# FFN-out in passes of 8, 8 and 6 units, and operands fetched by the places left for them

## The chip, the core and the metric

The kernel runs on one NeuronCore of a Trainium2 chip. The core has a matrix engine (TensorE, PE in the profile), a vector engine (VectorE, DVE), a scalar engine (ScalarE, ACT), a general engine (GpSimd, POOL) and a sequencer that issues most of the DMAs (SyncE, SP). Each works through its own queue in order, and semaphores tie the queues together. The metric is device time in microseconds (us) for one call. Working memory (SBUF) holds the operands, PSUM the sums of the matmuls.

## The reference

One decoder layer on 512 tokens, all in float32, with a residual stream x of width 2048:

```python
h = rmsnorm(x, attn_norm_g); proj = h @ w_in            # 2048 -> 9216
...                                                      # spatial gating, stick-breaking attention
x = x + merged @ w_o                                     # x1
h = rmsnorm(x, ffn_norm_g); hid = h @ w_ffn_in           # 2048 -> 2 * 5632
x = x + (jax.nn.silu(gate) * up) @ w_ffn_out             # 5632 -> 2048, x2
x = x + jax.nn.sigmoid(rmsnorm(x, ple_norm_g) @ w_ple_gate) * (p @ w_ple)
```

The change touches the last three of these products: FFN-in (`w_ffn_in`), FFN-out (`w_ffn_out`) and the gate (`w_ple_gate`).

## The kernel before

Activations lie transposed: features over the 128 partitions, tokens along the row. A *unit* is 256 features by 512 tokens, 1024 float32 in each partition. A product sums over units of its input and makes one *pair* (256 output features by 512 tokens) at a time; `j` counts the pairs of an output, eight of them for a width of 2048. FFN-in sums over 8 units and makes 44 pairs (`m`); FFN-out sums over 22 units of the hidden layer, and as the operands of 22 units don't fit in SBUF it does so in passes (`PASSES`, L33): 8, 7 and 7 units, each pass making all eight pairs, with the partial sums kept in DRAM (`spill["sum", j]`) between passes. The gate sums over 8 units again.

To get float32 accuracy from the faster float32r matmul, each operand is split into a high part (copied by ACT) and the rest (subtracted by DVE), and three matmuls make one product (`mm3`, L274; L280, L281 and L282 are its three matmuls): high by high, high by rest, rest by high. A unit's contribution to a pair is made in one of two forms:

- P, plain: four blocks of weights by two halves of the unit, 12 matmuls with 512 columns.
- S, after Strassen and Winograd: seven products of sums of quarters, 21 matmuls with 256 columns. FFN-in uses a variant of it for all its pairs but the first (L692, 14 matmuls, 7 of 512 and 7 of 256 columns).

The sums of weights that S needs are made on the fly: one by an accumulating DMA that POOL issues (L347), two by DVE (L359); ACT (L343) and DVE (L340) split the weights. Units go in doubles (`doubles`, L411) where two neighbours of one kind start at an even position; a unit left over goes singly, with weights of half the size. In FFN-out the second pass starts at unit 8 and the third at 15.

The operand of an S unit has seven quarters: the four plain ones and three sums. It takes one of eight *places* (3584 columns, high and rest) in an arena called `parts`; a P unit takes two blocks of 1024. Raw units, weights that land and whatever else is loaded live in a second arena, `wholes`, 13,312 columns. An S operand can be used as a plain one while its sums are not there yet: `PLAIN_UNTIL` (L34) says for each unit of a pass for how many pairs it is taken plain. In the kernel before, the first four units are taken plain for one pair and the others for two; in the gate and in FFN-in all units are taken plain for the first pair only.

A `Form` is such an operand in the making. `late_form` (L573) loads the unit, multiplies it by a gain where there is one (`gained`, L503, two ACT instructions at L504), and goes on with `plain_first` (L514): it splits the four plain quarters (L270 on ACT, L271 on DVE), gives the raw unit back, and later loads the same unit a *second* time, multiplies it by the gain again, makes the sums (`tt`, L509) and splits them. `all_first` (L551), which the first stage of the kernel uses, does all that from one load: the sums are made beside the plain quarters and split a little later.

What is fetched and built when is decided at every `tick` (L199), which comes twice in a double, and once in a single. A tick fetches one of the next three forms in `builds`, if there is room in `wholes`; it starts the next form if it has arrived and a place for it is left; and otherwise it fetches the second load of a form:

```python
        urgent = [f for f in seconds if f.used]
        for f in list(builds)[: 0 if urgent else AHEAD]:
            if not f.there and f.ready() and fits([(wholes, 1024, "old")]):
                f.fetch()
                break
        if builds and builds[0].ready() and builds[0].arrived() and fits(builds[0].sizes):
            builds.popleft().step()
        elif seconds and fits([(wholes, 5 * 256, "old")]):
            (urgent or seconds)[0].fetch_second()
```

The forms of the next pass enter `builds` ahead of the last pair of a pass, and those of the gate (`gs`) ahead of the last pair of the third pass. In that last pair each unit's place is given back when the unit has been used. The scheduler of the language then sets the order on every queue from dependences and estimated times; loads can be moved far ahead by it.

In the third pass a pair ends with its sum being added to the partial sum (L801), scaled (L1225), added to x1 (L1439) and written to DRAM as x2 (L1440); the third normalisation adds up its squares (L957, L961). The gate's operands are loaded from there (L500).

Of the kernel before, what the change touches and what calls it, by code (L numbers as in the profile page):

```python
# [19 lines left out]
P = 128  # L20
# [3 lines left out]
KU = D // (2 * P)  # L24
HID = 5632
KH = HID // P
# [3 lines left out]
EPS = 1e-6  # L30

OUT = "SSSSPPPP"
PASSES = 8, 7, 7  # L33
PLAIN_UNTIL = 1, 1, 1, 1, 2, 2, 2, 2  # L34
GATE = "SSSSSPPP"
PLACE = 7 * 256

AHEAD, WAIT = 3, 2
# [28 lines left out]
def hybrid_layer(  # L67
# [93 lines left out]
    def fits(sizes):  # L161

        before = parts.holes, wholes.holes
        parts.holes, wholes.holes = list(parts.holes), list(wholes.holes)
        try:
            for arena, n, how in sizes + [(wholes, 1024, "low")]:
                arena.take(n, how)
            return True
        except ValueError:
            return False  # L170
        finally:
            parts.holes, wholes.holes = before
# [26 lines left out]
    def tick():  # L199

        clock[0] += 1
        last, units = traced()[-1], dict(newest)
        urgent = [f for f in seconds if f.used]
        for f in list(builds)[: 0 if urgent else AHEAD]:
            if not f.there and f.ready() and fits([(wholes, 1024, "old")]):
                f.fetch()
                break
        if builds and builds[0].ready() and builds[0].arrived() and fits(builds[0].sizes):
# [3 lines that stand above are left out]
        while waiting and waiting[0][0] <= clock[0]:  # L212
            heapq.heappop(waiting)[2]()
        for i in reversed(traced()):
            if i is last:
                break
            if i.engine in units:
                tc.add_manual_dep(
                    i, units[i.engine],
                    mybir.DependencyInfo(mybir.DependencyClass.NoSync,  # L220
                                         mybir.DependencyReason.DATA),
                    reason="in its place among the units")
# [288 lines left out]
    def twice(x):  # L511
        return x.unsqueeze(1).to_broadcast([P, 2, 256])

    def plain_first(form, raw, gain=None):  # L514


        x = form.operand()
        split_into(x[:, 0:4, 0], x[:, 0:4, 1], cut(raw.f()))
        give(raw)
        form.at_plain = True  # L520
        seconds.append(form)
        yield
        while not form.second_arrived():
            yield
        w = form.second
        b = cut(w.f())
# [24 lines left out]
    def all_first(form, raw):  # L551


        b, s, v = cut(raw.f()), take(768, "old"), take(256, "old")
        t, x = cut(s.f()), form.operand()
        split_into(x[:, 0:4, 0], x[:, 0:4, 1], b)
        tt(t[:, 2], b[:, 3], b[:, 2])
        tt(v.f(), b[:, 3], b[:, 1])
        tt(t[:, 0], t[:, 2], b[:, 1])
        tt(t[:, 1], t[:, 0], b[:, 0], ALU.add)  # L560
        give(raw)
        form.at_plain = True
        yield
        yield
        split_into(x[:, 4:7, 0], x[:, 4:7, 1], t)
        give(s)
        yield
        while not form.used:
            yield
        split_into(x[:, 3, 0], x[:, 3, 1], v.f())  # L570
        give(v)

    def late_form(src, ready=always, gain=None, far=False):  # L573

        def steps(form):
            form.blocks = (parts.take(2 * PLACE, "place"),)
            w = form.raw()
            if gain:  # L580
                gained(w.f(), w.f(), *gain)
            yield
            yield from plain_first(form, w, gain)
            return form.operand()

        return Form("S", steps, [(parts, 2 * PLACE, "place")] + [(wholes, 1024, "low")], ready,
                    src, far)

    def strassen_form(src, ready=always, gain=None, raw=PLACE):

# [213 lines left out]
                    s = h[:, i * T : (i + 1) * T]  # L804
                    nc.vector.tensor_tensor(out=s, in0=s, in1=ps, op=ALU.add)

    def pair(forms, last=False, plain=None, parts_done=None, at=0, home=lambda: None,
             doubled=0):

        plain = plain or (0,) * len(forms)
        kinds = "".join("P" if n else f.kind for f, n in zip(forms, plain))
        p = Pair(kinds, home, doubled)
        for k, n in doubles(kinds, at):
            slot, ws = next_weights()
            fs = forms[k : k + n]
            p.add(kinds[k], ws, [f.plain() if plain[k] else f.get() for f in fs])
            for f, left in zip(fs, plain[k : k + n]):
                if left == 1:  # L820
                    f.use_plain()
                if last:
                    f.free()
            slots.append(slot)
            if parts_done and k + n == kinds.find("P"):
                last_parts(p, forms[k + n :], parts_done)
                break
        return p

    def plain_left(n, j, until=PLAIN_UNTIL):  # L830

        return tuple(max(0, u - j) for u in until[:n])

    def kinds_of(forms_kinds, j, until=PLAIN_UNTIL):
        return "".join("P" if left else k
                       for k, left in zip(forms_kinds, plain_left(len(forms_kinds), j, until)))

    def last_parts(p, forms, done):

# [435 lines left out]
    def plan_rest():  # L1275
        for j in range(KU):
            for b in "ba":
                plan((w_up_a if b == "a" else w_up_b)[j], "PPPP")
        for j in range(KU):
            plan(w_o[j], OUT)  # L1280
        for j in range(3, KU):
            planned.append((w_ple[j].rearrange("p (b c) -> p b c", b=4), 1, "P"))
        for m in range(KH):
            plan(w_ffn_in[m], ("S" if m else "P") * KU)
        at = 0
        for n in PASSES:
            for j in range(KU):
                plan(w_ffn_out[j], kinds_of("S" * n, j), at)
            at += n
        for j in range(KU):  # L1290
            plan(w_gate[j], GATE if j else "P" * KU)

    def y_form(c, i):
        return plain_form((lambda: y_a[i]) if c == "a" else lambda: load(y_spill[i]),
# [68 lines left out]
             for j in range(KU)}  # L1363
    there = set()

    def spilled_form(kind, n, j, gain=None):
        return (late_form if kind == "S" else plain_form)(
            lambda size=1024: load(spill[n, j], size), lambda: (n, j) in there, gain, far=True)

    fs = [spilled_form("S", "x1", j, (g_ffn, j)) for j in range(KU)]  # L1370
    raw = deque([load(xT[0])])
    for j in range(KU):
        if j < KU - 1:
# [14 lines left out]
    for j in range(5, 8):  # L1388
# [4 lines left out]

    spill.update({("hid", u): tc.dram_tile([P, 1024], F32, name=nm("hid"))
                  for u in range(KH // 2)})
    hs = [spilled_form("S", "hid", u) for u in range(KH // 2)]
    def hidden(m, o):
        g = o[:, :T]
        nc.vector.tensor_tensor(out=g, in0=g, in1=row2, op=ALU.mult)  # L1399
# [6 lines left out]

    for m in range(KH):
        if m == KH - 1:
            builds.extend(hs[: PASSES[0]])
        o = pair(fs, last=m == KH - 1, plain=(0 if m else 1,) * KU, doubled=7).out()  # L1410
        if m == 0:
            row2 = norm2.row()
        st = Staged(hidden(m, o))
        st.step()
        if m == KH - 1:
            st.get()
# [1 line left out]
    gs = [spilled_form(k, "x2", j, (g_ple, j)) for j, k in enumerate(GATE)]  # L1418
    norm3 = Norm()
    at = 0  # L1420
    for c, n in enumerate(PASSES):
        units, first = hs[at : at + n], at
        at += n
        for j in range(KU):
            if j == KU - 1:
                builds.extend(hs[at : at + PASSES[c + 1]] if c + 1 < len(PASSES) else gs)
            before = load(spill["sum", j]) if c else None
            x1 = load(spill["x1", j]) if c == len(PASSES) - 1 else None
            pr = pair(units, last=j == KU - 1, plain=plain_left(n, j), at=first)
            if before is None:  # L1430
                nc.sync.dma_start(out=spill["sum", j], in_=pr.out())
                continue
# [14 lines left out]
    for j in range(KU):  # L1447
# [18 lines left out]
            nc.sync.dma_start(out=outT[j][:, a:b], in_=s)  # L1466

        if j == KU - 1:
            pair(gs, parts_done=finish)
        else:  # L1470
            o = pair(gs, plain=(0 if j else 1,) * KU).out()
            row3 = norm3.row()
            finish(o, 0, 2 * T)
            give(e, x2)
# [87 lines left out]
```

## Time and profile before

| what | us |
|---|---|
| median of 3 runs | 2722.21 (2721.26 to 2723.8) |
| profiled execution, its own time | 2724.13 |
| its span, first to last instruction | 2722.2 |
| PE busy | 2668.2 (98%) |
| DVE busy | 2204.5 (81%) |
| ACT busy | 1405.6 (52%) |
| POOL busy | 477.3 (18%) |

Busy time is the time in which at least one instruction of the engine was running; matmuls overlap, so that their durations add up to more. The rows of a group give the engine, the line, the tiles written and read with their shape, how many there were, then their busy time in us and the mean duration of one in ns, then the idle time of the engine ahead of them and who ended it. "A <- B" in the waits means that engine and line A waited for B. A row of the chain of work gives start, duration and what ran. Along the time axis FFN-in runs from about 1190 to 2055 us, the passes of FFN-out from 2055, 2222 and 2364, and the gate from about 2525 to the end.

### The profile page before, as it was taken

What the parts mean: (1) busy time and instruction counts of PE and PEld (TensorE: products, weight loads), DVE (VectorE), ACT (ScalarE), POOL (GpSimd) and SP (SyncE); (2) the same over time, 40 slices, a digit from 0 to 9 for tenths busy, and PEclk for the clock granted to TensorE, in tenths of its full rate; (3) what the DMA queues carried; (4) which work ended last, traced back from release to release, by engine and by line L of the source; (5) the groups of instructions that cost most, each with busy time, mean ns of one, the idle gap of its engine ahead of it and who ended that gap; (6) DMA issues with size and microseconds to landing.
All of it is one profiled execution on the core that took longest, in us unless ns stands there. A gap on an engine that the chain in (4) does not pass through costs nothing.

```text
span 2722.2 us, 44416 instructions
## 1 busy us (share of the span) xinstructions
PE 2668.2 (98%) x16334; PEld 2374.5 (87%) x16334; DVE 2204.5 (81%) x3685; ACT 1405.6 (52%) x2174; POOL 477.3 (18%) x566
## 2 busy tenths in 40 slices
PE   8999999999999999999999999999999999989899
PEld 7888888888998889978888888888888999989698
DVE  8687878788887566679989898989889778789776
ACT  7656565655554343385444444444445444444643
POOL 0232323232210000011111111111111102111110
PEclk9999999999999999999999999999999999999899
DMA  7676777777775466688888888787878879889884
GB/s 227 155 189 167 189 167 190 167 200 180 178 189 193 131 181 200 172 268 209 205 229 201 207 195 215 195 209 195 206 193 263 245 223 283 252 238 277 253 234 124
DMA packets 305883, 557.74 MB, mean 205 GB/s; under 512 B 26752, under 2 KB 155648, under 8 KB 305664
## 3 DMA queue, kind: packets, MB, share of 16 engines
q1 hardware_dynamic: 242496, 447.52, 51.1%
q0 software_dynamic: 63168, 107.37, 24.7%
q8 instruction: 128, 2.10, 0.3%
q14 instruction: 91, 0.75, 0.1%
HBM read 507.61 MB, written 47.19 MB: 204 GB/s over the span
## 4 chain that ended last, share of the span: by engine, by line
PE 86%; DVE 6%; DMA 3%; ACT 2%; issue 2%; POOL 1%; SPq 0%; DVEq 0%; ACTq 0%; POOLq 0%
PE ps L692 40%; PE ps L281 13%; PE ps L282 13%; PE ps L280 13%; PE small L692 4%; DVE wlo L340 2%; DVE parts L271 1%; DVE out L751 1%; DMA wholes<-hid 1%; DMA wholes<-x 1%; PE small L1158 1%; ACT whi L343 1%; PE small L1033 1%; DVE wholes L509 1%; PE small L1108 1%
## 5 line engine op out<-in xcount | busy, mean ns | idle before, releaser
L343 ACT ACTIVATE whi<-wholes 128x1280 fp32r<-128x1280 f32 (+3 forms) x960 | 876.1, 927 | 805.6 <-DVE wholes L359 273.7
L692 PE MATMUL ps<-parts,whi 128*128 128x512 f32 x3384 | 1135.5, 398 | 3.3 <-ACT out L789 2.6
L340 DVE TENSOR_TENSOR wlo<-wholes,whi 128x1280 fp32r<-128x1280 f32 (+3 forms) x960 | 984.3, 1059 | 86.5 <-ACT whi L343 86.0
L281 PE MATMUL ps<-parts,whi 128*128 128x256 f32 (+1 forms) x2799 | 881.2, 315 | 11.1 <-DVE parts L271 10.8
L280 PE MATMUL ps<-parts,whi 128*128 128x256 f32 (+1 forms) x2782 | 869.5, 315 | 21.3 <-ACT parts L270 15.7
L282 PE MATMUL ps<-parts,wlo 128*128 128x256 f32 (+1 forms) x2799 | 878.6, 315 | 0.6 <-DVE wlo L340 0.6
L692 PEld LDWEIGHTS ps<-parts,wlo 128*128 128x128 f32 x3384 | 635.8, 188 | 142.0 <-issue 1.0
L692 PE MATMUL ps<-parts,wlo 128*128 128x256 f32 x3384 | 671.2, 279 | 0.0
L281 PEld LDWEIGHTS ps<-parts,whi 128*128 128x128 f32 x2799 | 536.5, 192 | 51.7 <-DVE parts L271 15.1
L280 PEld LDWEIGHTS ps<-parts,whi 128*128 128x128 f32 x2782 | 531.3, 192 | 57.2 <-ACT parts L270 18.5
L282 PEld LDWEIGHTS ps<-parts,wlo 128*128 128x128 f32 x2799 | 535.6, 192 | 33.1 <-DVE wlo L340 2.5
L692 PEld LDWEIGHTS ps<-parts,whi 128*128 128x128 f32 x3384 | 546.7, 189 | 9.8 <-ACT out L789 3.0
L359 DVE TENSOR_TENSOR wholes<-wholes 128x256 f32<-128x256 f32 (+1 forms) x840 | 348.2, 415 | 24.2 <-issue 3.5
L347 POOL DMA_DIRECT2D wholes<-w_ffn_in x172 | 149.7, 870 | 698.9 <-DVE wholes L359 261.5
L751 DVE TENSOR_TENSOR out<-out,ps 128x256 f32<-128x256 f32 x388 | 160.2, 415 | 125.1 <-ACT out L748 124.6
L347 POOL DMA_DIRECT2D wholes<-w_in x132 | 118.4, 898 | 489.3 <-DMA wholes<-w_in 112.6
L271 DVE TENSOR_TENSOR parts<-wholes,parts 128x1024 fp32r<-128x1024 f32 (+4 forms) x126 | 132.3, 1058 | 25.2 <-ACT parts L270 25.0
L347 POOL DMA_DIRECT2D wholes<-w_ffn_out x79 | 74.1, 939 | 403.3 <-DMA wholes<-w_ffn_out 152.6
L270 ACT ACTIVATE parts<-wholes 128x1024 fp32r<-128x1024 f32 (+4 forms) x126 | 113.7, 920 | 51.0 <-DVE wholes L509 35.9
L692 PE MATMUL small<-parts,whi 128*128 128x512 f32 x344 | 136.2, 397 | 0.0
L718 DVE TENSOR_TENSOR out<-out 128x256 f32<-128x256 f32 x144 | 61.0, 423 | 84.0 <-ACT out L715 81.5
L1400 ACT ACTIVATE out<-out 128x512 f32<-128x512 f32 x44 | 27.9, 633 | 161.1 <-DVE out L1399 161.1
(122 smaller groups left out, 1697.4 us busy)
## 6 DMA issues: line engine op xcount, KB each, us to landing
wholes<-w_ffn_in SPq DMA_DIRECT2D x172, 384.0 KB, 5.6
wholes<-w_in SPq DMA_DIRECT2D x132, 384.0 KB, 5.0
wholes<-w_ffn_in SPq DMA_DIRECT2D x172, 256.0 KB, 4.8
wholes<-w_ffn_in POOLq DMA_DIRECT2D x172, 256.0 KB, 5.4
wholes<-w_in SPq DMA_DIRECT2D x132, 256.0 KB, 4.1
wholes<-w_in POOLq DMA_DIRECT2D x132, 256.0 KB, 4.9
wholes<-w_ffn_out SPq DMA_DIRECT2D x65, 384.0 KB, 5.3
wholes<-x SPq DMA_DIRECT2D x45, 512.0 KB, 5.5
```

What stands on the lines that cost most here:

```text
L270: return (nc.scalar.activation(hi, src, AF.Copy), nc.vector.tensor_tensor(out=lo, in0=src, in1=hi.bitcast(F32), op=ALU.subtract))
L271: nc.vector.tensor_tensor(out=lo, in0=src, in1=hi.bitcast(F32), op=ALU.subtract))
L280: nc.tensor.matmul(ps, sh, mh, start=start, stop=False)
L281: nc.tensor.matmul(ps, sh, ml, start=False, stop=False)
L282: return nc.tensor.matmul(ps, sl, mh, start=False, stop=stop)
L340: in_turn(nc.vector.tensor_tensor(out=self.lo[:, blocks], in0=r, in1=h.bitcast(F32), op=ALU.subtract))
L343: in_turn(nc.scalar.activation(h, r, AF.Copy))
L347: nc.gpsimd.dma_start(out=raw[:, 3:5], in_=self.src[:, 1:3], accum_op=ALU.add)
L359: in_turn(nc.vector.tensor_tensor(out=o, in0=x, in1=y, op=ALU.add))
L692: m = nc.tensor.matmul(out, l, r, start=first and k == 0, stop=last and k == 1)
L718: in_turn(nc.vector.tensor_tensor(out=out, in0=x, in1=y, op=op))
L751: in_turn(nc.vector.tensor_tensor(out=out, in0=x, in1=y, op=op))
```

## The change

- `PASSES` becomes three strings of kinds: eight S units, eight S units, and four S with two P. The third pass now starts at unit 16. There are no single units in FFN-out any more.
- `PLAIN_UNTIL` becomes a table for each pass: as before in the first two; in the third the four S units are taken plain for two pairs. `GATE_UNTIL` is new: in the gate, units 2, 3 and 4 are taken plain for two pairs.
- A tick fetches a form ahead only if a place in `parts` is left for it and for those ahead of it in the queue, or if `wholes` has room for three more raw blocks.
- The operands of FFN-in are made by `all_first`, from one load, and keep two blocks of `wholes` asked for instead of one; `all_first` loses one of its two bare yields.
- The forms of the gate enter `builds` at the start of the third pass instead of ahead of its last pair.
- `plain_left` and `kinds_of` give way to `now`, which says the kinds of a pair.

```diff
@@
-PASSES = 8, 7, 7
-PLAIN_UNTIL = 1, 1, 1, 1, 2, 2, 2, 2
+PASSES = "SSSSSSSS", "SSSSSSSS", "SSSSPP"
+PLAIN_UNTIL = (1, 1, 1, 1, 2, 2, 2, 2), (1, 1, 1, 1, 2, 2, 2, 2), (2, 2, 2, 2, 1, 1)
 GATE = "SSSSSPPP"
+GATE_UNTIL = 1, 1, 2, 2, 2, 1, 1, 1
@@ tick
         urgent = [f for f in seconds if f.used]
+        sizes = []
         for f in list(builds)[: 0 if urgent else AHEAD]:
-            if not f.there and f.ready() and fits([(wholes, 1024, "old")]):
+            sizes += [s for s in f.sizes if s[0] is parts]
+            raw = [(wholes, 1024, "old")]
+            if not f.there and f.ready() and (fits(sizes + raw) or fits(raw * 3)):
                 f.fetch()
                 break
@@ all_first
         form.at_plain = True
         yield
-        yield
         split_into(x[:, 4:7, 0], x[:, 4:7, 1], t)
@@
-    def late_form(src, ready=always, gain=None, far=False):
+    def late_form(src, ready=always, gain=None, far=False, twice=True):
...
-            yield from plain_first(form, w, gain)
+            yield from plain_first(form, w, gain) if twice else all_first(form, w)
             return form.operand()
...
-        return Form("S", steps, [(parts, 2 * PLACE, "place")] + [(wholes, 1024, "low")], ready,
-                    src, far)
+        return Form("S", steps, [(parts, 2 * PLACE, "place")]
+                    + [(wholes, 1024, "low")] * (1 if twice else 2), ready, src, far)
@@ pair
-        plain = plain or (0,) * len(forms)
-        kinds = "".join("P" if n else f.kind for f, n in zip(forms, plain))
+        until = until or (0,) * len(forms)
+        kinds = now("".join(f.kind for f in forms), until, j)
...
+    def now(kinds, until, j):
+
+        return "".join("P" if j < n else k for k, n in zip(kinds, until))
@@ plan_rest
-        for n in PASSES:
+        for kinds, until in zip(PASSES, PLAIN_UNTIL):
             for j in range(KU):
-                plan(w_ffn_out[j], kinds_of("S" * n, j), at)
-            at += n
+                plan(w_ffn_out[j], now(kinds, until, j), at)
+            at += len(kinds)
         for j in range(KU):
-            plan(w_gate[j], GATE if j else "P" * KU)
+            plan(w_gate[j], now(GATE, GATE_UNTIL, j))
@@
-    fs = [spilled_form("S", "x1", j, (g_ffn, j)) for j in range(KU)]
+    fs = [spilled_form("S", "x1", j, (g_ffn, j), twice=False) for j in range(KU)]
@@
-    for c, n in enumerate(PASSES):
-        units, first = hs[at : at + n], at
-        at += n
+    for c, units in enumerate(hs):
+        first, at = at, at + len(units)
+        if c == len(hs) - 1:
+            builds.extend(gs)
         for j in range(KU):
-            if j == KU - 1:
-                builds.extend(hs[at : at + PASSES[c + 1]] if c + 1 < len(PASSES) else gs)
+            if j == KU - 1 and c < len(hs) - 1:
+                builds.extend(hs[c + 1])
...
-            pr = pair(units, last=j == KU - 1, plain=plain_left(n, j), at=first)
+            pr = pair(units, last=j == KU - 1, j=j, until=PLAIN_UNTIL[c], at=first)
@@ gate
         if j == KU - 1:
-            pair(gs, parts_done=finish)
+            pair(gs, j=j, until=GATE_UNTIL, parts_done=finish)
         else:
-            o = pair(gs, plain=(0 if j else 1,) * KU).out()
+            o = pair(gs, j=j, until=GATE_UNTIL).out()
```

More of the change, by code (lines that the diff above doesn't have):

```diff
@@ L512, in twice, with plain_first @@
         return x.unsqueeze(1).to_broadcast([P, 2, 256])
-    def plain_first(form, raw, gain=None):
+    def plain_first(form, raw, gain):
         x = form.operand()
@@ L805, in onto, with pair @@
                     nc.vector.tensor_tensor(out=s, in0=s, in1=ps, op=ALU.add)
-    def pair(forms, last=False, plain=None, parts_done=None, at=0, home=lambda: None,
-             doubled=0):
-        plain = plain or (0,) * len(forms)
-        kinds = "".join("P" if n else f.kind for f, n in zip(forms, plain))
+    def pair(forms, last=False, j=0, until=None, parts_done=None, at=0,
+             home=lambda: None, doubled=0):
+        until = until or (0,) * len(forms)
+        kinds = now("".join(f.kind for f in forms), until, j)
         p = Pair(kinds, home, doubled)
@@ L817, in pair @@
             fs = forms[k : k + n]
-            p.add(kinds[k], ws, [f.plain() if plain[k] else f.get() for f in fs])
-            for f, left in zip(fs, plain[k : k + n]):
-                if left == 1:
+            p.add(kinds[k], ws, [f.plain() if j < until[k] else f.get() for f in fs])
+            for f, m in zip(fs, until[k : k + n]):
+                if j == m - 1:
                     f.use_plain()
@@ L828, in pair @@
         return p
[L830 to L836, printed above, removed]
+    def now(kinds, until, j):
+        return "".join("P" if j < n else k for k, n in zip(kinds, until))
     def last_parts(p, forms, done):
@@ L1364, in hybrid_layer, with spilled_form @@
     there = set()
-    def spilled_form(kind, n, j, gain=None):
+    def spilled_form(kind, n, j, gain=None, **how):
         return (late_form if kind == "S" else plain_form)(
-            lambda size=1024: load(spill[n, j], size), lambda: (n, j) in there, gain, far=True)
-    fs = [spilled_form("S", "x1", j, (g_ffn, j)) for j in range(KU)]
+            lambda size=1024: load(spill[n, j], size), lambda: (n, j) in there, gain, far=True,
+            **how)
+    fs = [spilled_form("S", "x1", j, (g_ffn, j), twice=False) for j in range(KU)]
     raw = deque([load(xT[0])])
@@ L1395, in hybrid_layer @@
                   for u in range(KH // 2)})
-    hs = [spilled_form("S", "hid", u) for u in range(KH // 2)]
+    hs = []
+    for kinds in PASSES:
+        hs.append([spilled_form(k, "hid", u)
+                   for u, k in enumerate(kinds, sum(map(len, hs)))])
     def hidden(m, o):
@@ L1408, in hybrid_layer @@
         if m == KH - 1:
-            builds.extend(hs[: PASSES[0]])
-        o = pair(fs, last=m == KH - 1, plain=(0 if m else 1,) * KU, doubled=7).out()
+            builds.extend(hs[0])
+        o = pair(fs, last=m == KH - 1, j=m, until=(1,) * KU, doubled=7).out()
         if m == 0:
```

## The prediction

> **What bounds the kernel now.** I read the page first, then the busy time of each engine by stage, then what PE waits for in the stages where it idles, then the counts of matmuls there, and last the chain of work through the worst gap.
>
> ```profile
> span 2722.2 us, 44416 instructions
> PE 2668.2 (98%) x16334; PEld 2374.5 (87%) x16334; DVE 2204.5 (81%) x3685; ACT 1405.6 (52%) x2174; POOL 477.3 (18%) x566
> ...
> wholes<-x SPq DMA_DIRECT2D x45, 512.0 KB, 5.5
> ```
>
> PE is the bound: 98% of the span. So only two things can move the time, the matmuls that PE runs and the places where it stands still. The stages (the first number after the window is its length, then the busy time of PE, PEld, DVE, ACT and POOL, the granted clock and the DMA share and GB/s):
>
> ```profile
> 1190.00:1240.00 50.00, 46.96 (x233) 39.07 (x232) 42.48 (x73) 37.03 (x52) 7.89 (x9) 0.97 0.83 239
> 2054.90:2100.00 45.10, 43.86 (x235) 37.84 (x234) 41.99 (x69) 24.08 (x30) 4.35 (x5) 1.00 0.87 268
> 2222.00:2265.00 43.00, 43.00 (x258) 38.40 (x257) 38.58 (x65) 21.21 (x26) 5.62 (x6) 1.00 0.90 275
> 2364.00:2435.00 71.00, 60.63 (x355) 54.45 (x355) 59.36 (x97) 30.15 (x39) 9.93 (x10) 0.94 0.85 246
> 2435.00:2500.00 65.00, 65.00 (x534) 64.50 (x534) 62.55 (x99) 30.52 (x40) 13.78 (x15) 0.99 0.97 278
> 2522.00:2584.00 62.00, 48.69 (x239) 39.00 (x238) 45.40 (x66) 38.73 (x52) 8.90 (x8) 0.89 0.83 252
> ```
>
> These are the starts of FFN-in, of the three passes and of the gate, and (fifth) the third pass in its steady state. PE idles 3.0 us at FFN-in, 1.2 at pass one, nothing at pass two, 10.4 at pass three, 13.3 at the gate. What it waits for, in the windows of FFN-in, of pass three (two rows) and of the gate (two rows):
>
> ```profile
> PE ps L692 <- ACT out L789: 2.6, 1, 2.6
> ...
> PE ps L280 <- ACT parts L270: 6.4, 3, 2.9
> PE ps L281 <- DVE parts L271: 4.0, 2, 3.3
> ...
> PE ps L281 <- DVE parts L271: 5.1, 6, 2.3
> PE ps L280 <- ACT parts L270: 4.0, 3, 3.5
> ```
>
> L270 and L271 split operands, so the two large gaps are operands not ready. They cost more than their idle time, because matmuls after a gap start at a slower pace. After the 3.3 us gap of pass three (start, duration):
>
> ```profile
> 2389.71 0.41 PE L281 MATMUL ps<-parts,whi 128*128 128x256 f32 x1
> 2389.92 0.41 PE L282 MATMUL ps<-parts,wlo 128*128 128x256 f32 x1
> ...
> 2391.93 0.28 PE L280 MATMUL ps<-parts,whi 128*128 128x256 f32 x1
> 2392.05 0.28 PE L281 MATMUL ps<-parts,whi 128*128 128x256 f32 x1
> ```
>
> A start every 0.21 us, and 2 us later one every 0.12. To price a transition whole I count its matmuls at the undisturbed pace. The first rows below are that pace, from 2100 to 2200 us for 256 columns and from 2054.9 to 2076.6 for 512 (the two partner lines have 32 each as well); then the counts in the windows of pass three and of the gate:
>
> ```profile
> L280 PE MATMUL ps<-parts,whi 128*128 128x256 f32 x279 | 79.0, 283 | 0.0
> L281 PE MATMUL ps<-parts,whi 128*128 128x256 f32 x279 | 79.0, 283 | 0.0
> L282 PE MATMUL ps<-parts,wlo 128*128 128x256 f32 x278 | 78.7, 283 | 0.0
> ...
> L280 PE MATMUL ps<-parts,whi 128*128 128x512 f32 x32 | 12.5, 389 | 0.0
> ...
> L280 PE MATMUL ps<-parts,whi 128*128 128x256 f32 x79 | 22.7, 308 | 6.4 <-ACT parts L270 6.4
> L282 PE MATMUL ps<-parts,wlo 128*128 128x512 f32 x40 | 15.7, 392 | 0.0
> ...
> L281 PE MATMUL ps<-parts,whi 128*128 128x512 f32 x35 | 15.5, 443 | 4.5 <-DVE parts L271 4.2 <-DVE parts L619 0.3
> L280 PE MATMUL ps<-parts,whi 128*128 128x256 f32 x41 | 11.6, 318 | 4.7 <-ACT parts L270 4.0 <-ACT whi L343 0.7
> ```
>
> 100 us / 836 = 0.120 us for 256 columns, 21.7 / 96 = 0.226 for 512. Pass three: 3 x 79 x 0.120 + 3 x 40 x 0.226 = 55.5 of 71.0 us, so 15.5 lost. Gate: 3 x 41 x 0.120 + 3 x 35 x 0.226 = 38.5 of 62.0, so 23.5 lost (some 1 of it the normalisation's sixteen small matmuls, an estimate).
>
> By the Trainium skill (TensorE: Matmul & The Clock Gate, "What's actually happening") the array's clock halves after an idle window of about 3.4 us and is whole again after as long a busy one; with that, a removed gap would bring up to 1.7 us beyond its own length (an estimate from the page's figures). The slow stretch above agrees in kind, about 2 us at little over half the pace; my counts already hold it.
>
> **The change, part by part.**
>
> *More plain units: +3.8.* A plain unit costs 12 x 0.226 = 2.71 us, an S unit 21 x 0.120 = 2.52, so each unit and pair that turns plain costs 0.20 us (0.19 by the rounded figures). Before, FFN-out has 12 + 10 + 10 = 32 of them; after, 12 + 12 + (4 x 2 + 2 x 8) = 48. The gate gets 3 more. 19 x 0.20 = 3.8 us on PE, with nothing to hide it.
>
> *FFN-in from one load: -2.5.* Eight loads (of the 45 of x) and sixteen gains at L504 go; the gains would have run on ACT in the very stretch where PE waits 2.6 us for ACT's copy L789. The sums and splits on DVE stay and move earlier, into a window where DVE is busy 42.5 of 50 us; the last operand still waits for the last x1. I keep 0.5 of the 3.0 idle. Bounds: nothing gained, or all 3.0 and a slow start of some 1.5.
>
> *Pass two with eight units: +1.5.* It starts like pass one, eight places to be freed and four second loads due by the next pair, where PE lost 1.2. Bounds: 0 (pass two now) and 15.5 (pass three now). Nearest is pass one, with partial sums to be loaded on top.
>
> *Pass three with four S and two P: -13.5.* The gap comes with the second pair. Its S units need their second loads, and these get their blocks late (the chain of work, and the DVE rows that go with the steady state further down):
>
> ```profile
> 2372.49 9.30 DMA wholes<-hid
> ...
> 2539.05 6.73 DMA x<-wholes
> 2545.83 6.51 DMA wholes<-x
> ...
> 2552.37 0.73 ACT parts L504
> 2553.13 1.41 DVE parts L619 x2
> ```
>
> The first row is that load: DVE waits for it to land at 2381.8, with its other work queued behind. After, there are four second loads instead of seven, due at the third pair instead of four at the second; two plain pairs of 6 x 2.71 = 16.3 us give them 32 us where there were 19. I leave 2.0 of the 15.5. Bounds 0 and 15.5. The rule on fetching ahead works the same way here: no raw block lies in `wholes` waiting for a place while a second load needs the room.
>
> *The gate's forms from the start of pass three: -16.5.* Four S units take places 0 to 3; the two P take 4 x 1024 columns from column 14336 on, which ends at 18432 and cuts into the sixth place. So places six and seven (from 21504) are left whole: two gate forms can be built during pass three, splits, second loads and all. The others come in the last pair as now, but units 2 to 4 need their sums one pair later. What stays is x2 of the last pair: its chain is in the rows above, write 6.7, load 6.5, gain 0.7, split 0.7 or so, and ahead of it the tail of the pair on DVE, at least five instructions of the sizes shown below (about 5 us; I take 8, since weights are split between them). That is 22.5 us from the pair's end; PE reaches that unit after 7 x 2.71 = 19.0. So some 3.5 us of waiting, about 2 of slow start, 1 for the normalisation and 0.5 for the rest: 7.0 stays of 23.5. Bounds: 23.5 stays, or 1.
>
> *DVE and the DMAs in pass three: +2.0.* Now the cover is thin. DVE is busy 62.55 of 65 us, 16.9 in a pair of 17.6, and the DMA share is 0.97. The durations:
>
> ```profile
> 2442.13 2.08 DVE L340 TENSOR_TENSOR wlo<-wholes,whi 128x1280 fp32r<-128x1280 f32 x2
> 2441.79 0.42 DVE L359 TENSOR_TENSOR wholes<-wholes 128x256 f32<-128x256 f32 x1
> 2450.28 0.61 DVE L359 TENSOR_TENSOR wholes<-wholes 128x128 f32<-128x128 f32 x2
> 2450.81 1.15 DVE L340 TENSOR_TENSOR wlo<-wholes,whi 128x640 fp32r<-128x640 f32 x2
> 2432.35 1.22 DVE L271 TENSOR_TENSOR parts<-wholes,parts 128x1024 fp32r<-128x1024 f32 x1
> 2415.58 0.95 DVE L271 TENSOR_TENSOR parts<-wholes,parts 128x768 fp32r<-128x768 f32 x1
> 2439.73 0.68 DVE L718 TENSOR_TENSOR out<-ps,out 128x512 f32<-128x512 f32 x1
> ```
>
> A pair loses one double of S weights (2.08 + 2 x 0.42 = 2.9) and the single (1.15 + 0.61 = 1.8), gains a double of P weights (1.2, taken as the 1024-wide split) and, since S and P sums now meet at the end, two additions of 0.68 for one of 0.42 and one of 0.68 (+0.3): 16.9 - 4.7 + 1.5 = 13.7 of a pair of 4 x 2.52 + 2 x 2.71 = 15.5 us. Six such pairs leave 11 us; the two gate forms want 2 x (1.22 + 0.95 + 4 x 0.42) = 7.7. It fits, at 96%, as full as now; I put 2.0 on it. Bounds 0 and 7.7.
>
> **The sum** against the profiled execution's 2724.1: + 3.8 - 2.5 + 1.5 - 13.5 - 16.5 + 2.0 = 2698.9, so 2699, 0.9% less. The median of the runs shown is 2722.2, 1.9 below the profiled one, which the range takes in.
>
> **The rivals.**
>
> *Slower: fresh blocks block the queues.* x2 of a pair is loaded for the gate one pair after it was made. SP has to wait until the write has landed (6.73 us) before it issues the load (6.51), and the loads of weights stand behind; ACT's gain then waits, with the splits of weights behind it. Against it: that chain is in the trace only at the gate's start, and the scheduler may put the load later. If both early forms are uncovered: 2 x 13.2 = 26.5 idle, and at the gate's ratio of lost to idle time (23.5 / 13.3 = 1.77) 47 us: 2746. It decides from 28.7 us (2727.6 - 2699), some 16 of idle: more than one of the two loads. The Trainium skill speaks for its first half (DMA: Bandwidth & Descriptors, "Two DMAs through the same engine are not ordered"): a DMA that reads what another wrote needs the first one's semaphore, and it is the issuing engine that waits. The 6.73 us row shows such a wait.
>
> *The gap moves from pass three to pass two.* Pass two then has eight second loads, and partial sums in `wholes` beside them. If it takes over the 15.5 us, the time is 2699 + 14 = 2713. For it: this is what pass three has now, with seven units. Against it: pass one does eight with 1.2.
>
> *The early start brings nothing.* If no place or no room in `wholes` is found for the gate's forms, its 16.5 stay and only the rest is won: 2715.5; with a loss at pass two as well, no change.
>
> **How the numbers follow.** Forecast, 2687 to 2711: 0.62. The gap moves: 0.13. Nothing from the early start: 0.08, half of it within 0.2%. Fresh blocks: 0.14. All transitions nearly free (below 2687): 0.03. A measurement of this kernel tells about 0.2% from no change, 5.4 us: 2716.8 to 2727.6. Faster: 0.62 + 0.03 + 0.10 of the moved gap, rounded to 0.75; same 0.09; slower 0.16. The range takes in the two middle cases: 2687 to 2725.
>
> **What would show it.** PE's waits at L270 and L271 ahead of the third pass nearly gone, and at the gate one wait for the last x2 left; 37 loads of x; 15 fewer accumulating loads for FFN-out (64 doubles of S for 65 doubles and 14 singles); gains at L504 during pass three. I am wrong if PE idles inside the third pass, if ACT stands at L504 for a load there, or if the second pass starts with gaps over 5 us.

## The result, and the profile after

The changed kernel takes 2695.16 us (median of 4 runs, 2693.25 to 2698.13) against 2723.01 for the kernel before: a ratio of 0.9894, 95% interval 0.9875 to 0.9914. The forecast was 2699, faster. The profiled execution took 2693.36. Line numbers have moved by three or four: L274 and L275 split operands, L284 to L286 are the three matmuls of `mm3`, L347 and L344 split weights, L508 is the gain.

The page after, and two rows of its DMA issues:

```profile
span 2691.7 us, 43830 instructions
PE 2657.5 (99%) x16168; PEld 2360.8 (88%) x16168; DVE 2180.3 (81%) x3631; ACT 1385.6 (51%) x2137; POOL 456.8 (17%) x549
...
wholes<-x SPq DMA_DIRECT2D x37, 512.0 KB, 5.5
wholes<-w_ffn_out POOLq DMA_DIRECT2D x64, 256.0 KB, 5.4
```

37 loads of x and 64 accumulating loads (15 fewer) are as forecast. The busy time of each engine by stage (columns as in the prediction) follows, first before, then after. The rows are the three passes and the gate, and each begins where PE starts the 512-wide plain matmuls of a stage's first pair:

```profile
2054.90:2220.40 165.50, 164.26 (x1239) 158.24 (x1238) 131.32 (x209) 79.82 (x96) 22.61 (x26) 1.00 0.84 241
2220.40:2363.80 143.40, 143.40 (x1089) 138.50 (x1088) 121.02 (x199) 68.17 (x89) 25.21 (x26) 1.00 0.92 264
2363.80:2524.30 160.50, 150.13 (x1090) 143.29 (x1089) 143.67 (x228) 76.19 (x98) 25.39 (x26) 0.97 0.90 263
2524.30:2722.20 197.90, 179.03 (x1125) 160.08 (x1123) 144.80 (x221) 90.40 (x120) 23.04 (x22) 0.96 0.69 201
```

```profile
2049.40:2213.50 164.10, 164.09 (x1238) 158.19 (x1237) 131.16 (x208) 79.84 (x96) 22.68 (x26) 1.00 0.86 242
2213.50:2378.20 164.70, 164.39 (x1239) 158.07 (x1238) 134.51 (x210) 77.30 (x93) 21.80 (x25) 1.00 0.87 259
2378.20:2511.70 133.50, 128.29 (x800) 115.16 (x799) 116.68 (x169) 63.46 (x79) 10.47 (x12) 1.00 0.83 261
2511.70:2691.70 180.00, 171.57 (x1097) 155.83 (x1096) 134.56 (x205) 81.89 (x109) 19.96 (x20) 1.00 0.71 210
```

| stage | before | after | difference |
|---|---|---|---|
| up to FFN-out | 2054.9 | 2049.4 | -5.5 |
| pass one | 165.5 | 164.1 | -1.4 |
| passes two and three | 303.9 | 298.2 | -5.7 |
| gate to the end | 197.9 | 180.0 | -17.9 |

The sum, -30.5, is the difference of the two spans. PE's idle time in the four rows fell from 1.2, 0, 10.4 and 18.9 us to 0, 0.3, 5.2 and 8.4; in the gate 5.6 us before and 5.4 after are the end of the kernel, behind PE's last matmul. What PE waits for after, in the third pass (three rows) and in the gate up to 2600 us (two):

```profile
PE ps L284 <- ACT parts L274: 3.2, 2, 1.9
PE ps L286 <- DVE wlo L344: 1.1, 1, 1.1
PE ps L285 <- DVE parts L275: 0.5, 1, 0.5
...
PE ps L285 <- DVE parts L275: 1.5, 1, 1.5
PE small L944 <- DVE diag L942: 0.8, 1, 0.8
```

The operand waits of the third pass, 10.4 us at L270 and L271 before, are 3.7; those of the gate, 9.1 in the two rows that the prediction shows, are 1.5.

### The profile page after: what moved, and what is told of

Read it like the earlier page. It is cut to its first block, busy times and chain, and to the rows that moved or that the text cites. A ratio compares the mean times of both kernels' runs of the same rounds, so it can differ in the third digit from the quotient of the medians.

```text
span 2691.7 us, 43830 instructions
## 1 busy us (share of the span) xinstructions
PE 2657.5 (99%) x16168; PEld 2360.8 (88%) x16168; DVE 2180.3 (81%) x3631; ACT 1385.6 (51%) x2137; POOL 456.8 (17%) x549
## 4 chain that ended last, share of the span: by engine, by line
PE 85%; DVE 6%; DMA 3%; ACT 3%; issue 2%; POOL 1%; SPq 0%; DVEq 0%; ACTq 0%; POOLq 0%
PE ps L695 40%; PE ps L285 13%; PE ps L286 13%; PE ps L284 13%; PE small L695 4%; DVE wlo L344 2%; DVE out L754 1%; DMA wholes<-x 1%; PE small L1157 1%; ACT whi L347 1%; DMA wholes<-w_in 1%; DVE wholes L363 1%; PE small L1032 1%; DMA wholes<-w_gate 0%; DVE wholes L513 0%
## 5 line engine op out<-in xcount | busy, mean ns | idle before, releaser
L347 ACT ACTIVATE whi<-wholes 128x512 fp32r<-128x512 f32 (+3 forms) x933 | 866.1, 941 | 798.9 <-DVE wholes L363 255.1
L344 DVE TENSOR_TENSOR wlo<-wholes,whi 128x512 fp32r<-128x512 f32 (+3 forms) x933 | 973.8, 1078 | 94.8 <-ACT whi L347 94.5
L285 PE MATMUL ps<-parts,whi 128*128 128x256 f32 (+1 forms) x2742 | 869.2, 317 | 2.7 <-DVE parts L275 2.5
L284 PE MATMUL ps<-parts,whi 128*128 128x256 f32 (+1 forms) x2720 | 858.2, 317 | 11.9 <-ACT parts L274 9.4
L286 PE MATMUL ps<-parts,wlo 128*128 128x256 f32 (+1 forms) x2742 | 867.7, 318 | 1.6 <-DVE wlo L344 1.6
L695 PEld LDWEIGHTS ps<-parts,wlo 128*128 128x128 f32 x3384 | 635.5, 188 | 142.6 <-issue 1.0
L285 PEld LDWEIGHTS ps<-parts,whi 128*128 128x128 f32 x2742 | 521.5, 190 | 44.5 <-DVE parts L275 5.9
L284 PEld LDWEIGHTS ps<-parts,whi 128*128 128x128 f32 x2720 | 516.8, 190 | 48.8 <-ACT parts L274 11.3
L286 PEld LDWEIGHTS ps<-parts,wlo 128*128 128x128 f32 x2742 | 521.4, 190 | 35.6 <-DVE wlo L344 2.2
L695 PEld LDWEIGHTS ps<-parts,whi 128*128 128x128 f32 x3384 | 545.0, 189 | 4.9 <-issue 1.0
L363 DVE TENSOR_TENSOR wholes<-wholes 128x256 f32<-128x256 f32 (+1 forms) x806 | 338.8, 420 | 23.4 <-issue 6.2
L351 POOL DMA_DIRECT2D wholes<-w_ffn_in x172 | 150.0, 872 | 689.9 <-DVE wholes L363 246.9
L351 POOL DMA_DIRECT2D wholes<-w_in x132 | 118.1, 897 | 489.5 <-DMA wholes<-w_in 141.8
L275 DVE TENSOR_TENSOR parts<-wholes,parts 128x1024 fp32r<-128x1024 f32 (+4 forms) x134 | 131.3, 990 | 18.7 <-ACT parts L274 18.7
L274 ACT ACTIVATE parts<-wholes 128x1024 fp32r<-128x1024 f32 (+4 forms) x134 | 112.7, 864 | 41.6 <-DVE wholes L513 21.5
L351 POOL DMA_DIRECT2D wholes<-w_ffn_out x64 | 55.8, 872 | 403.9 <-DMA wholes<-w_ffn_out 154.0
L1403 ACT ACTIVATE out<-out 128x512 f32<-128x512 f32 x44 | 27.9, 633 | 159.2 <-DVE out L1402 159.2
```

The lines of the kernel that those rows point to most:

```text
L274: return (nc.scalar.activation(hi, src, AF.Copy), nc.vector.tensor_tensor(out=lo, in0=src, in1=hi.bitcast(F32), op=ALU.subtract))
L275: nc.vector.tensor_tensor(out=lo, in0=src, in1=hi.bitcast(F32), op=ALU.subtract))
L284: nc.tensor.matmul(ps, sh, mh, start=start, stop=False)
L285: nc.tensor.matmul(ps, sh, ml, start=False, stop=False)
L286: return nc.tensor.matmul(ps, sl, mh, start=False, stop=stop)
L344: in_turn(nc.vector.tensor_tensor(out=self.lo[:, blocks], in0=r, in1=h.bitcast(F32), op=ALU.subtract))
```

## The experiments

All totals are medians with the ratio to the kernel before and its 95% interval. Stage lengths come from one profiled execution each. How far they can be trusted: the changed kernel and its ten variants with the single load have the same source for FFN-in (two of them with another rule on fetching ahead), and FFN-out starts between 2046.3 and 2051.9 us in them; the totals of the changed kernel alone spread over 5 us. So I rest nothing on a stage difference under about 5 us.

**The gate's forms queued late again.**

```diff
-        if c == len(hs) - 1:
-            builds.extend(gs)
...
-            if j == KU - 1 and c < len(hs) - 1:
-                builds.extend(hs[c + 1])
+            if j == KU - 1:
+                builds.extend(hs[c + 1] if c < len(hs) - 1 else gs)
```

> The changed kernel, but the gate's forms enter the queue ahead of the last pair of the third pass again, as before. Theory 1 (the early forms carry the gate's gain): the gate's 17.8 us are mostly lost, +12 to +18, so 2707 to 2713, with PE waiting on L274 and L275 in the gate's first two pairs. Rival (taking units 2 to 4 plain in the second pair carries it, early forms or not): +0 to +5, 2695 to 2700.

Measured: 2692.17 (0.9879, 0.9865 to 0.9893). Third pass and gate:

```profile
2379.10:2510.50 131.40, 128.53 (x800) 115.96 (x799) 113.18 (x162) 58.56 (x73) 10.44 (x12) 0.99 0.83 260
2510.50:2692.10 181.60, 172.41 (x1097) 155.41 (x1095) 138.44 (x210) 86.84 (x114) 20.30 (x20) 0.99 0.73 212
```

The gate keeps its gain (181.6 against 180.0) without the early forms. Theory 1 falls; the rival holds.

**One plain pair in the gate.**

```diff
-GATE_UNTIL = 1, 1, 2, 2, 2, 1, 1, 1
+GATE_UNTIL = 1, 1, 1, 1, 1, 1, 1, 1
```

> The changed kernel, but every unit of the gate is taken plain for the first pair only. Theory 1 (early forms carry it): -0.6 us of matmuls and some 0 to 4 of new waits for the second loads of units 2 to 4, 2694 to 2699. Rival (the second plain pair carries it): +8 to +10, 2703 to 2705, the waits of the gate's second pair back.

Measured: 2713.23 (0.9955, 0.9941 to 0.9968), 18 us more than the changed kernel. The gate's row, and what PE waits for in it up to 2600:

```profile
2510.60:2708.20 197.60, 176.08 (x1124) 160.38 (x1123) 137.89 (x210) 83.00 (x111) 22.10 (x22) 0.94 0.68 194
```

```profile
PE ps L284 <- ACT parts L274: 8.1, 2, 6.7
PE small L944 <- DVE diag L942: 5.9, 1, 5.9
```

197.6 us is the gate of the kernel before (197.9), early forms and all. The rival holds, and by twice its size. One wait of 6.7 us is for a split of a second load. In the other, of 5.9 us, PE, in order, stands at the normalisation's small matmul (L944) until DVE has made its operand, the tile `diag`. DVE in turn stands idle for 6.1 us until GpSimd has made `cols` (L978). GpSimd, DVE, and then GpSimd in the changed kernel:

```profile
2533.03 0.86 POOL L351 DMA_DIRECT2D wholes<-w_gate  x1 [4.03 <-issue]
2533.59 1.36 POOL L978 TENSOR_TENSOR cols<-mean,expo 128x4 f32<-128x4 f32 x1
...
2534.99 0.29 DVE L942 TENSOR_SCALAR diag<-ident,cols 128x128 f32<-128x128 f32 x1 [6.09 <-POOL cols L978]
...
2530.44 1.04 POOL L978 TENSOR_TENSOR cols<-mean,expo 128x4 f32<-128x4 f32 x1 [14.12 <-DVE mean L975]
2531.44 0.91 POOL L351 DMA_DIRECT2D wholes<-w_gate  x1
```

With one plain pair the sums of weights for units 2 to 4 are due a pair earlier, and GpSimd issues five of the gate's accumulating loads (L351) ahead of L978; it stood 4.0 us at the fifth, for what the profile does not show. In the changed kernel one such load is ahead of it, and L978 runs as soon as DVE's mean is there. Both of PE's waits are short or gone in the changed kernel and with late forms, where units 2 to 4 are plain twice. The granted clock of the row is 0.94, against 1.00 in the changed kernel. That agrees in kind with the Trainium skill (TensorE: Matmul & The Clock Gate, "What's actually happening"), by which the array's clock is halved after an idle window of about 3.4 us: both of these waits are longer, and none of the changed kernel's in this row is. Behind each of the two the matmuls start at little over half the pace for some 4 to 6 us (512 columns every 0.43 us, not 0.23). As a limit the 3.4 us are not what these runs show: in `old_rule_late` below, the matmuls of the gate start every 0.43 us behind a wait of only 1.9.

**Both gate parts undone** (the two diffs above together).

> The changed kernel with both gate parts undone: forms queued ahead of the last pair, all units plain for one pair. Theory 2: as with the early forms and one plain pair, gate stage 195 to 200 us, 2709 to 2714. Theory 1 in a weaker form (early forms matter where there is one plain pair): 5 to 10 us slower still, 2717 to 2724.

Measured: 2713.71 (0.9956, 0.9944 to 0.9969), gate 200.5 us. Theory 2, the second plain pair, holds: with one plain pair the early forms don't matter either. The wait at L944 is there again, 6.5 us, and again GpSimd issues accumulating loads ahead of L978.

**The second plain pair alone, in the kernel before.**

```diff
+GATE_UNTIL = 1, 1, 2, 2, 2, 1, 1, 1
...
-            plan(w_gate[j], GATE if j else "P" * KU)
+            plan(w_gate[j], kinds_of(GATE, j, GATE_UNTIL))
...
-            o = pair(gs, plain=(0 if j else 1,) * KU).out()
+            o = pair(gs, plain=plain_left(KU, j, GATE_UNTIL)).out()
```

> The kernel before, with one part of the change: units 2, 3 and 4 of the gate are taken plain for two pairs. Theory 2 (formed after the first runs: the second plain pair carries the gate's gain by itself, the early forms nothing): the gate's stage falls from 197.9 to 180 to 183 us, the run to 2706 to 2710. Theory 3 (it needs the small third pass too, which leaves VectorE and the DMAs free at the change of stages): no more than 6 us, 2717 to 2723.

Measured: 2714.57 (0.996, 0.9947 to 0.9974).

```profile
2525.10:2710.00 184.90, 174.11 (x1097) 156.46 (x1096) 141.89 (x218) 89.31 (x119) 20.05 (x20) 0.99 0.72 212
```

The gate falls by 13.0 of the 17.9 us with the three lines alone. That lies between the two expectations and nearer to theory 2. The total is 11.8 less than the 2726.41 of the kernel before measured beside it, which fits the 13.0; taken as it stands, 2714.57 is nearer to theory 3's 2717 to 2723, because the kernel before took 3 us longer beside it than when the expectation was worked out.

**FFN-in from two loads again.**

```diff
-    fs = [spilled_form("S", "x1", j, (g_ffn, j), twice=False) for j in range(KU)]
+    fs = [spilled_form("S", "x1", j, (g_ffn, j)) for j in range(KU)]
```

> The changed kernel, but the operands of FFN-in are loaded twice again. Theory 1 (the single load brings the 5.4 us that the changed kernel is ahead by at the start of FFN-out): +5.4, 2700 to 2701, PE waiting for ACT's copy early in FFN-in. Rival (the rule on fetching ahead brings it): no change, 2695.

Measured: 2709.25 (0.9938, 0.9925 to 0.9951), 14 us more, not 5.4. FFN-out starts at 2054.1, 4.7 us later, the size that theory 1 has; that is a small difference for one execution, but later than in any of the eleven kernels above. Between 1180 and 1300 us PE's waits are 3.9 us, against 0.7 in the changed kernel and 4.4 in the kernel before. The longest, 2.2 us, is for a split by ACT (L274), not for the copy that theory 1 names. The rest comes in stages whose source was not touched, pass one and the gate:

```profile
2054.10:2224.20 170.10, 166.21 (x1239) 159.21 (x1238) 132.89 (x213) 81.52 (x99) 22.63 (x26) 0.99 0.84 240
2519.70:2705.60 185.90, 175.19 (x1098) 159.64 (x1096) 135.00 (x209) 81.93 (x111) 20.29 (x20) 0.97 0.69 203
```

6.0 and 5.9 us over the changed kernel. In pass one PE waits 3.9 us for splits by DVE (L275), in the gate once 4.6 us for a split of weights by ACT (L347); the changed kernel has nothing and 0.3 us there. Why an edit upstream brings these waits stays open; that the scheduler's order shifts further down is the obvious guess, and wasn't shown.

**The old rule on fetching ahead.**

```diff
-            if not f.there and f.ready() and (fits(sizes + raw) or fits(raw * 3)):
+            if not f.there and f.ready() and fits(raw):
```

> The changed kernel with the old rule on fetching ahead (room in the arena of raw blocks is enough). Theory (raw blocks that wait for a place hold back the second loads): the second and third pass lose 3 to 10 us more, 2698 to 2705, with waits at L274 and L275 in their second pairs. Rival (the sizes of the passes and the plain pairs did it): within 3 us of 2695.

Measured: 2691.77 (0.9877, 0.9863 to 0.989). Third pass 132.8, gate 177.3 us. With the early forms beside it the rule brings nothing here; the rival holds.

**Old rule and late gate forms together.**

> The changed kernel without the new rule on fetching ahead and without the early gate forms: what is left of the change are the passes, the plain pairs and the single load of FFN-in. If neither of the two brings anything: 2688 to 2693, no slower than the changed kernel's 2695. Rival (each makes up for the lack of the other): 2698 to 2705.

Measured: 2707.31 (0.9935, 0.9921 to 0.9948): 15 us worse than either alone. The rows are the third pass and the gate:

```profile
2380.20:2512.90 132.70, 128.58 (x801) 117.02 (x800) 113.67 (x162) 60.20 (x73) 11.33 (x13) 0.97 0.83 255
2512.90:2705.60 192.70, 179.56 (x1097) 161.67 (x1095) 138.68 (x209) 86.23 (x113) 19.44 (x19) 0.95 0.67 196
```

The rival holds again, a little beyond its range: the third pass is the same, and it is the gate that loses 11 to 15 us against the two runs with one of them undone. So either of the new rule and the early start keeps the gate's start short, and neither adds to the other. How they do it stays open.

**The third pass, plain for one pair.**

```diff
-PLAIN_UNTIL = ..., (2, 2, 2, 2, 1, 1)
+PLAIN_UNTIL = ..., (1, 1, 1, 1, 1, 1)
```

> The changed kernel, but the four S units of the third pass are taken plain for one pair only. Matmuls: 4 x 0.2 = -0.8 us. Theory (the second plain pair gives the four second loads their time): the third pass takes 139 to 145 us instead of 133.5, with a wait at L274 or L275 ahead of its second pair, 2700 to 2706. Rival (fewer S units are enough): 2693 to 2696.

Measured: 2702.38 (0.992, 0.9906 to 0.9933). The third pass, and its main wait:

```profile
2377.80:2520.20 142.40, 132.10 (x837) 120.58 (x836) 123.61 (x177) 66.35 (x82) 10.44 (x12) 0.96 0.83 253
```

```profile
PE ps L284 <- ACT parts L274: 7.4, 3, 3.3
```

8.9 us more than with two plain pairs, with 0.8 us less of matmuls: the theory holds, second loads need the time. One of the three waits, 2.2 us, is still in the first pair, and the changed kernel has it too (1.9); the other two are ahead of 256-wide products.

**Six S units in the third pass,** plain for two pairs, with the gate's forms early and late.

```diff
-PASSES = "SSSSSSSS", "SSSSSSSS", "SSSSPP"
+PASSES = "SSSSSSSS", "SSSSSSSS", "SSSSSS"
-PLAIN_UNTIL = ..., (2, 2, 2, 2, 1, 1)
+PLAIN_UNTIL = ..., (2, 2, 2, 2, 2, 2)
```

> The changed kernel with six S units in the third pass, all taken plain for two pairs, so that none is plain from the third pair on. Matmuls alone: 2 units x 6 pairs x 0.19 to 0.20 = -2.4 us, 2693. Theory (VectorE is the cover that gets thin: 1.7 us more weight work a pair of 15.1 us, and six second loads instead of four): it loses more than that, 2697 to 2703. Rival (VectorE has room): 2692 to 2694, the plain units bought nothing.

> Six S units in the third pass, taken plain for two pairs, and the gate's forms queued late. With the early forms the third pass took 148.5 us against 133.5 with two P units. Theory 4 (early forms on a full VectorE): third pass 133 to 137, the run 2698 to 2706. Theory 5 (the weights and second loads of the two more S units are the cost, early forms or not): third pass 142 or more, 2708 to 2715.

Measured: 2716.86 (0.9966, 0.9953 to 0.9978) and 2719.61 (0.998, 0.9971 to 0.9989). The third pass, early and late, and the gate, late:

```profile
2378.70:2527.20 148.50, 132.72 (x902) 123.61 (x901) 127.15 (x189) 66.94 (x82) 15.67 (x18) 0.94 0.83 250
...
2379.50:2520.00 140.50, 128.75 (x901) 121.23 (x900) 120.28 (x178) 62.02 (x75) 15.66 (x18) 0.96 0.85 254
2520.00:2717.70 197.70, 177.31 (x1098) 158.31 (x1096) 143.91 (x218) 90.87 (x119) 21.12 (x20) 0.97 0.69 204
```

2.4 us of matmuls saved, 15.0 lost in the pass with the early forms, 9.1 without (against 131.4). So within the pass the early forms cost 8.0 us where there are six S units, and nothing that one execution can show where there are four (2.1): theory 4 has part of it, theory 5 the larger part, and the 140.5 lies between both. The two plain units are worth far more than their matmuls cost. With them gone the gate loses too (186.2 against 180.0 with early forms, 197.7 against 181.6 with late ones), which neither theory foresaw. Over the whole kernel the early forms therefore do not cost here: the run without them is 2.7 us slower, and outside both expectations.

**Passes of 8, 7 and 7 with the rest of the change,** gate forms early and late.

```diff
-PASSES = "SSSSSSSS", "SSSSSSSS", "SSSSPP"
-PLAIN_UNTIL = (1, 1, 1, 1, 2, 2, 2, 2), (1, 1, 1, 1, 2, 2, 2, 2), (2, 2, 2, 2, 1, 1)
+PASSES = "SSSSSSSS", "SSSSSSS", "SSSSSSS"
+PLAIN_UNTIL = (1, 1, 1, 1, 2, 2, 2, 2), (1, 1, 1, 1, 2, 2, 2), (1, 1, 1, 1, 2, 2, 2)
```

> The changed kernel, but with passes of 8, 7 and 7 S units and the plain pairs of before. Theory 1 (units and plain pairs carry the third pass): the third pass loses some 15 us at its start again, 3.2 of matmuls are saved, one gate form fewer is early: 2703 to 2711. Rival (the rule on fetching ahead cures the third pass whatever the passes): 2690 to 2695.

> Passes of 8, 7 and 7 S units with the rest of the change, and the gate's forms queued ahead of the last pair again. With the early forms the third pass took 181.8 us (160.5 in the kernel before) and the run 2739. Theory 4 (in a third pass whose VectorE is full, the early forms are what costs 20 us): the third pass is back at 158 to 163, the run at 2705 to 2721. Rival (the rule on fetching ahead costs it): third pass 175 or more, 2730 to 2740.

Measured: 2739.2 (1.0049, 1.0035 to 1.0062) and 2742.39 (1.0072, 1.006 to 1.0085), slower than the kernel before. The third pass and the gate of the second, and PE's waits in that pass:

```profile
2355.90:2533.80 177.90, 154.47 (x1089) 145.31 (x1088) 146.96 (x225) 77.11 (x97) 25.39 (x26) 0.91 0.83 239
2533.80:2740.00 206.20, 180.87 (x1098) 160.79 (x1096) 142.21 (x215) 89.82 (x118) 19.95 (x20) 0.93 0.67 192
```

```profile
PE ps L284 <- ACT parts L274: 21.3, 5, 6.9
```

The third pass takes 177.9 us where the same units took 160.5 before, and the early forms are not why (181.8 with them). Of the parts of the change left in that kernel, the new rule on fetching ahead is the one that acts in that pass, so it is the suspect; it wasn't run alone. The gate, too, is no shorter than the 197.9 before, or hardly (206.2, and 196.9 with early forms), in spite of its second plain pair. Theory 1 missed its 2703 to 2711 by 28 us, the rival beside it (the rule cures the third pass) by more, and theory 4 fell; the rival of the second run, with its 175 or more and 2730 to 2740, is close.

## Why the prediction was right

The time is 4 us from the forecast, and the fall, 27.9 us in the medians and 30.8 between the two profiled executions, is near the 25.2 of the sum. The sums by stage agree too: -2.5 for FFN-in (measured -5.5, and -1.4 in pass one, for which nothing was forecast); +3.2 + 1.5 - 13.5 + 2.0 = -6.8 for passes two and three (measured -5.7); +0.6 - 16.5 = -15.9 for the gate (measured -17.9). But the largest term was right for a wrong reason, so that its agreement is in part luck.

- *More plain units, +3.8.* Not measured by itself. What the runs show is its other side: the two plain units of the third pass are worth 9 to 15 us there, presumably because the weights and second loads of two S units need not be made.
- *FFN-in, -2.5.* Right in kind, and mis-sized: I had the slow start behind the idle time in the bounds and left it out of the forecast. PE's waits between 1180 and 1300 us fell from 4.4 to 0.7, and the copy that PE waited for is no longer among them (nor is it with two loads; the longest wait there is 2.2 us, for a split). Undone alone, this part costs 14 us in the total, 9 of them downstream, where I had forecast nothing and the cause stays open.
- *Pass two, +1.5.* 164.7 us against pass one's 164.1: 0.6. The rival in which the gap moves to pass two did not come true; PE idles 0.3 us there.
- *Pass three, -13.5, and DVE in it, +2.0.* Six plain units for two pairs and six pairs of 15.5 make 125.5 us; measured 133.5. So 8.0 are still lost where I left 4.0 in all. Two plain pairs instead of one are worth 8.9, as argued. The longest wait that is left, 1.9 us, is not for a second load: it is in the first pair, where ACT stood 3.3 us until a first load of a hidden unit had landed, which my working did not have. The early forms cost 2.1 (133.5 against 131.4), which is the 2.0 that I put on DVE, but a difference that one execution can't carry. The sentence that the rule on fetching ahead helps here is not borne out: without it the pass takes 132.8.
- *The gate, -16.5.* This is the step that failed. "Two gate forms can be built during pass three" was given as the reason; without it the gate takes 181.6 us instead of 180.0, and with it but one plain pair 197.6. The part named beside it, that units 2 to 4 need their sums one pair later, carries 13.0 alone and some 18 in the changed kernel. The early forms are not nothing either: where the old rule on fetching ahead is back, the gate is 15.4 us longer without them. And x2 of the last pair is not waited for, though I had 3.5 us and a slow start for it: PE does other work first. In the timeline of the changed kernel it turns from the 512-wide plain matmuls of the first pair to the 256-wide ones of the second, and only later back:

```profile
2525.12 0.39 PE L286 MATMUL ps<-parts,wlo 128*128 128x512 f32 x1
2525.76 0.39 PE L284 MATMUL ps<-parts,whi 128*128 128x256 f32 x1 [0.25 <-ACT whi L347]
...
2533.71 0.40 PE L286 MATMUL ps<-parts,wlo 128*128 128x512 f32 x1
2533.95 0.40 PE L284 MATMUL ps<-parts,whi 128*128 128x512 f32 x1
```

  The scheduler put S products of the second pair ahead of the first pair's last plain units. It does so with one plain pair as well, so this is not what the second one brings.
- *Fresh blocks, the slower rival.* The gains do run in the third pass and ACT does stand ahead of them, on loads of x2:

```profile
2412.63 1.34 ACT L508 ACTIVATE wholes<-wholes,gcol 128x512 f32<-128x512 f32 x2 [1.90 <-DMA wholes<-x]
2432.09 1.34 ACT L508 ACTIVATE wholes<-wholes,gcol 128x512 f32<-128x512 f32 x2 [0.96 <-DMA wholes<-x]
```

  1.9 and 1.0 us, and 0.8 at a third, not 13 for each, too short to reach PE.
- *The signs.* Two things that were to say "I am wrong" did come: PE idles inside the third pass (5.2 us), and ACT stands at the gain for a load there. Neither sign named a size, and neither effect was large enough to undo the gain.

No kernel run here is clearly faster than the changed one: 0.9877 and 0.9879 with one part undone, against 0.9894, lie within its interval.

## What to carry to other kernels

Where an operand is used in a cheap form first and in a costly one later, the time between the two is what to tune: one more round of the cheap form cost 0.2 us a unit on the matrix engine (an estimate from the pace of the matmuls) and made one stage 9 us shorter and another 13 to 18. Price a transition whole, by its matmuls at the undisturbed pace, and then test each part of a change by undoing it alone and with another: here two parts that seemed worth nothing each were worth 15 us together, and a sum that came out right hid a cause that was wrong. A part measured beside one set of sizes says little about another: parts that went with a gain of 28 us at passes of 8, 8 and 6 went with a loss of 15 to 18 at 8, 7 and 7.

## What was not expected

The normalisation's eight small matmuls can cost as much as an operand: in the two runs with the changed passes and one plain pair in the gate PE stood 5.9 and 6.5 us at L944, where it stood 0.8 in the changed kernel. PE goes on in order, DVE was late with a 128x128 tile, and DVE was late because GpSimd had loads of weights to issue ahead of an instruction of 1.4 us on four columns. So where loads are moved, it is worth asking what small work stands behind them in the queue that issues them.
